# Rotating an 8192 x 8192 float32 matrix by 90 degrees: macro tiles of 3072 columns with three load and three store buffers, in place of tiles of 4096 columns with two and two

## The chip, the cores and the metric

The kernel runs on one core of one Trainium2 chip. The time is the device time of that core in microseconds (us), lower is better. "Packet" means one record of the DMA part of the trace: one contiguous piece that one of the core's 16 DMA engines reads and writes on, or the few bytes that report a completion.

## The reference

```python
def setup_inputs():
    return {"x": np.random.randn(8192, 8192).astype(np.float32), "k": 1}

def reference(x, k):
    return np.rot90(x, k)
```

There is nothing to compute: 268.44 MB are read and 268.44 MB are written. A rotation by 90 degrees is a transpose and a reversal of one axis.

## The kernel before

A macro tile is 1024 rows by C columns. It is loaded in blocks of 128 rows (RT = 8 blocks, q of them in one DMA). DVE (VectorE) copies each block into small chunks of 128 x 512 with the columns of each 128-block reversed; PE (TensorE) transposes 128 x 128 blocks into its output memory, PSUM; ACT (ScalarE) copies PSUM into a store buffer of four column blocks (G = 4), and a DMA writes that out. Loads are issued by SP (SyncE), stores by ACT: two queues over the same 16 engines.

```python
R = 1024; RT = R // P; W = 4096; CH = 512; G = 4; PW = 2
# whole_reads: a finalize hook that makes each store read its 16 KB per partition
# as one contiguous piece, though it writes four rows of 4 KB:
#     ap = [ap[0], [1, 1], [1, ap[1][1] * ap[2][1]]]
# macro_tiles: widths 4096, 4096; in the last strip 4096, 2048, 1024, 1024
a_pool = ctx.enter_context(tc.tile_pool(name="a_pool", bufs=2))   # loads
r_pool = ctx.enter_context(tc.tile_pool(name="r_pool", bufs=68))  # chunks
o_pool = ctx.enter_context(tc.tile_pool(name="o_pool", bufs=2))   # stores
...
for r0, c0, C in tiles:
    q = W // C
    for t0 in range(0, RT, q):
        a = o_pool.tile(...) if loads < 2 else a_pool.tile(...)
        loads += 1
        nc.sync.dma_start(out=a, in_=x[...])             # 2 MB
        ...                                              # DVE: chunks[t, j] <- a, reversed
    for g0 in range(0, C // P, G):
        ot = o_pool.tile([P, W], dt, tag="o")
        for h in range(0, G, PW):
            ...                                          # PE: needs chunks of ALL t (8 row blocks)
            nc.scalar.copy(o[...], ps[:])
            ...
            nc.scalar.dma_start(out=dst, in_=o[...])     # 2 MB
```

Of the kernel before, what the change touches and what calls it, by code (L numbers as in the profile page):

```python
# [2 lines left out]

# [5 lines left out]

P = 128  # L10




R = 1024
RT = R // P
W = 4096
CH = 512
G = 4
PW = 2  # L20


def whole_reads(nc):






    for fn in nc.m.functions:  # L30
        for block in fn.blocks:
            for n, ins in enumerate(block.instructions):
                if not isinstance(ins, mybir.InstDMACopy):
                    continue
                src = ins.ins[0]
                ap = [list(d) for d in src.ap]
                if len(ap) == 3 and ap[2][0] == 1 and ap[1][0] == ap[2][1]:
                    ap = [ap[0], [1, 1], [1, ap[1][1] * ap[2][1]]]
                    block.instructions[n] = copy.replace(
                        ins,  # L40
                        ins=[copy.replace(src, ap=ap)],
                        ant_dge_precooked=False,
                    )


def macro_tiles(N, M):

    for r0 in range(0, N, R):
        widths = [W] * (M // W)
        if r0 == 0:  # L50
            widths[:1] = [4096]
        if r0 + R == N:
            widths[-1:] = [2048, 1024, 1024]
        c0 = 0
        for C in widths:
            yield r0, c0, C
            c0 += C


@with_exitstack  # L60
def kernel(
    ctx: ExitStack,
    tc: tile.TileContext,
    x: bass.AP,
    k: bass.AP,
    out: bass.AP,
):
    nc = tc.nc
    assert k == 1, f"only k=1 supported, got {k}"
    nc.at_finalize(whole_reads)  # L70

    N, M = x.shape
    dt = x.dtype

    consts = ctx.enter_context(tc.tile_pool(name="consts", bufs=1))
    ident = consts.tile([P, P], dt)
    make_identity(nc, ident)

    a_pool = ctx.enter_context(tc.tile_pool(name="a_pool", bufs=2))
    r_pool = ctx.enter_context(tc.tile_pool(name="r_pool", bufs=68))  # L80
    o_pool = ctx.enter_context(tc.tile_pool(name="o_pool", bufs=2))
    psum_pool = ctx.enter_context(
        tc.tile_pool(name="psum", bufs=2, space=bass.MemoryType.PSUM)
    )

    tiles = list(macro_tiles(N, M))
    loads = 0
    for r0, c0, C in tiles:
        last = (r0, c0, C) == tiles[-1]
        q = W // C  # L90
        chunks = {}
        for t0 in range(0, RT, q):

            if loads < 2:
                a = o_pool.tile([P, W], dt, tag="o")
            else:
                a = a_pool.tile([P, W], dt, tag="a")
            loads += 1
            a = a.rearrange("r (q c) -> r q c", q=q)
            nc.sync.dma_start(  # L100
                out=a,
                in_=x[r0 + t0 * P : r0 + (t0 + q) * P, c0 : c0 + C].rearrange(
                    "(q r) c -> r q c", q=q
                ),
            )


            for u in range(q):
                for j in range(C // CH):
                    ar = r_pool.tile([P, CH // P, P], dt, tag="ar")  # L110
                    nc.vector.tensor_copy(  # L111
                        out=ar[:],
                        in_=a[:, u, j * CH : (j + 1) * CH].rearrange(
                            "r (b m) -> r b m", m=P
                        )[:, :, ::-1],
                    )
                    chunks[t0 + u, j] = ar

        for g0 in range(0, C // P, G):
            ot = o_pool.tile([P, W], dt, tag="o")  # L120
            o = ot.rearrange("m (g f) -> m g f", g=G)
            S = PW if last and g0 + G == C // P else G
            for h in range(0, G, PW):
                ps = psum_pool.tile([P, PW, R], mybir.dt.float32)
                for w in range(PW):
                    g = g0 + h + w
                    for t in range(RT):
                        nc.tensor.transpose(  # L128
                            ps[:, PW - 1 - w, t * P : (t + 1) * P],
                            chunks[t, g * P // CH][:, g % (CH // P), :],  # L130
                            ident,
                        )
                nc.scalar.copy(o[:, G - PW - h : G - h, :], ps[:])  # L133

                done = h + PW
                if done % S == 0:
                    top = M - c0 - (g0 + done) * P
                    dst = out[top : top + S * P, r0 : r0 + R].rearrange(
                        "(g m) f -> m g f", g=S
                    )  # L140
                    nc.scalar.dma_start(  # L141
                        out=dst, in_=o[:, G - done : G - done + S, :]
                    )


# [1 line left out]
_INS = ['x', 'k']  # L147
_OUTS = [((8192, 8192), 'float32')]

_NUMBERS = {'k': 1}  # L150


# [26 lines left out]
```

## Time and profile before

| | before |
|---|---|
| time, median | 1276.11 us |
| PE, ACT, DVE busy | 56, 37, 28% |
| DMA queues, share of 16 engines | 49.8% loads, 49.8% stores |
| rate from 100 to 1100 us | 428 GB/s |

Part of the profile page of the kernel before: busy time by engine, the rate in 40 equal slices of the span, and the DMA queues (q1 is the loads' queue, q10 the stores'; packets, MB, share of 16 engines' span).

```profile
PE 719.2 (56%) x4096; PEld 685.5 (54%) x4096; DVE 355.2 (28%) x1024; ACT 466.9 (37%) x257; POOL 0.7 (0%) x6
...
GB/s 375 366 427 427 427 428 431 429 428 428 430 428 430 428 427 429 429 429 429 427 427 427 429 427 428 427 427 429 428 427 426 424 423 429 427 425 422 420 408 338
...
q1 hardware_dynamic: 20480, 268.44, 49.8%
q10 hardware_dynamic: 18576, 268.44, 49.8%
```

The rate is flat at 427 to 431 in the first three quarters after the start and at 420 to 429 after that; it is low in the first two slices and in the last two. The two queues together cover 99.6% of the engines.

The longest waits of the kernel before (us in total, times, longest):

```profile
DVE ar L111 <- DMA a<-in_x_dram: 894.4, 128, 15.4
ACT ot L133 <- DMA out_dram<-ot: 733.5, 122, 11.4
```

The compute engines wait for DMA on both sides: DVE for each of the 128 loads, ACT for 122 stores to give a buffer back.

The DMA view of the kernel before between 300 and 360 us (same columns as above):

```profile
q10 hardware_dynamic: 878, 12.80, 50.2%
q1 hardware_dynamic: 880, 12.85, 50.0%
```

The busy table by stretches of the kernel before (last three columns: granted PE clock, DMA share, GB/s):

```profile
0.00:100.00 100.00, 34.94 (x192) 30.55 (x192) 36.07 (x104) 20.08 (x12) 0.70 (x6) 0.88 0.96 391
100.00:1100.00 1000.00, 583.64 (x3264) 559.44 (x3264) 283.05 (x816) 370.49 (x204) 0.00 (x0) 0.75 1.01 428
1180.00:1274.00 94.00, 51.52 (x360) 48.42 (x358) 16.65 (x48) 43.22 (x24) 0.00 (x0) 0.81 0.94 390
```

### The profile page before, as it was taken

The numbers are of one execution on the slowest core, as the hardware profiler recorded it, in microseconds if no ns is written. First come the engines' busy times: TensorE is split into PE (matmuls) and PEld (weight loads), VectorE is DVE, ScalarE is ACT, GpSimd is POOL, SyncE is SP. The second block draws the span as 40 slices with busy tenths as digits, with TensorE's granted clock in tenths as the row PEclk, the third lists the DMA queues.
The fourth block names the chain that finished last, engine by engine and source line by source line (L and its number), as shares of the span: only waits on it lengthen the run. The fifth ranks groups of instructions, "written<-read, shape, count | busy, mean of one in ns | idle before, by whom it ended". The sixth has DMA issues, their size and how long they took to land.

```text
span 1274.2 us, 10388 instructions
## 1 busy us (share of the span) xinstructions
PE 719.2 (56%) x4096; PEld 685.5 (54%) x4096; DVE 355.2 (28%) x1024; ACT 466.9 (37%) x257; POOL 0.7 (0%) x6
## 2 busy tenths in 40 slices
PE   1455556556655665556546565565565665665564
PEld 0355556555554655556546555565555554665564
DVE  4422232223222322232223222322232222321210
ACT  0233343334334333343334333433343333434444
POOL 0000000000000000000000000000000000000000
PEclk9968686877777677776886867768777778678878
DMA  9999999999999999999999999999999999999998
GB/s 375 366 427 427 427 428 431 429 428 428 430 428 430 428 427 429 429 429 429 427 427 427 429 427 428 427 427 429 428 427 426 424 423 429 427 425 422 420 408 338
DMA packets 39105, 537.55 MB, mean 422 GB/s; under 512 B 4112, under 2 KB 4112, under 8 KB 6160
## 3 DMA queue, kind: packets, MB, share of 16 engines
q1 hardware_dynamic: 20480, 268.44, 49.8%
q10 hardware_dynamic: 18576, 268.44, 49.8%
q8 instruction: 32, 0.52, 0.2%
q14 instruction: 17, 0.14, 0.0%
HBM read 268.44 MB, written 268.44 MB: 421 GB/s over the span
## 4 chain that ended last, share of the span: by engine, by line
DMA 84%; DVE 12%; issue 2%; ACT 1%; PE 0%; DVEq 0%; SPq 0%; ACTq 0%
DMA a<-in_x_dram 81%; DVE ar L111 12%; DMA out_dram<-ot 3%; ACT ot L133 1%; PE ps L128 0%; DVEq L111 0%; SPq L100 0%; ACTq L133 0%; ACTq L141 0%
## 5 line engine op out<-in xcount | busy, mean ns | idle before, releaser
L128 PE MATMUL ps<-ident,ar 128*128 128x128 f32 x4096 | 719.2, 358 | 543.8 <-ACT ot L133 500.2
L128 PEld LDWEIGHTS ps<-ident,ar 128*128 128x128 f32 x4096 | 685.5, 192 | 577.3 <-ACT ot L133 530.5
L133 ACT COPY ot<-ps 128x2048 f32<-128x2048 f32 x256 | 465.6, 1870 | 789.3 <-DMA out_dram<-ot 733.5
L111 DVE COPY ar<-a 128x512 f32<-128x512 f32 x1024 | 355.2, 421 | 894.4 <-DMA a<-in_x_dram 894.4
L133 ACT ACT_TABLE_LOAD x1 | 1.3, 1283 | 10.9 <-DVE ar L111 10.9
masks.py:199 POOL TENSOR_SCALAR_AFFINE_SELECT ident<-ident 128x128 f32<-128x128 f32 x1 | 0.3, 292 | 0.1
masks.py:197 POOL MEMSET ident<- 128x128 f32 x1 | 0.2, 204 | 0.3 <-POOLq L160 0.3
L160 POOL MEMSET const-bfloat16-1.0<- 128x1 bf16 x1 | 0.1, 102 | 0.0
L160 POOL MEMSET const-uint8-127<- 128x1 uint8 x1 | 0.1, 102 | 0.0
L160 POOL MEMSET const-float32-0.0<- 128x1 f32 x1 | 0.1, 99 | 0.2 <-issue 0.2
L160 POOL MEMSET const-float32-1.0<- 128x1 f32 x1 | 0.1, 99 | 0.0
## 6 DMA issues: line engine op xcount, KB each, us to landing
a<-in_x_dram SPq DMA_DIRECT2D x128, 2048.0 KB, 16.6
out_dram<-ot ACTq DMA_DIRECT2D x127, 2048.0 KB, 15.9
out_dram<-ot ACTq DMA_DIRECT2D x2, 1024.0 KB, 5.7
```

The costliest lines, as they stand in the source:

```text
L111: nc.vector.tensor_copy(out=ar[:], in_=a[:, u, j * CH : (j + 1) * CH].rearrange("r (b m) -> r b m", m=P)[:, :, ::-1],)
L128: nc.tensor.transpose(ps[:, PW - 1 - w, t * P : (t + 1) * P], chunks[t, g * P // CH][:, g % (CH // P), :], ident,)
L133: nc.scalar.copy(o[:, G - PW - h : G - h, :], ps[:])
L160: nc = _bacc.Bacc("TRN2", target_bir_lowering=False, num_devices=1)
```

## The change

The intent was more transfers in flight: smaller load buffers (12 KB per partition instead of 16) make room for three load and three store buffers. Core of the diff:

```diff
-W = 4096
+W = 3072
-        widths = [W] * (M // W)
+        widths = [3072, 3072, 2048]
         if r0 == 0:
-            widths[:1] = [4096]
+            widths = [2048, 3072, 3072]
         if r0 + R == N:
-            widths[-1:] = [2048, 1024, 1024]
+            widths = [3072, 3072, 1024, 1024]
...
-            yield r0, c0, C
+            yield r0, c0, C, max(1, 2048 // C)
...
-    a_pool = ctx.enter_context(tc.tile_pool(name="a_pool", bufs=2))
-    r_pool = ctx.enter_context(tc.tile_pool(name="r_pool", bufs=68))
-    o_pool = ctx.enter_context(tc.tile_pool(name="o_pool", bufs=2))
+    a_pool = ctx.enter_context(tc.tile_pool(name="a_pool", bufs=3))
+    r_pool = ctx.enter_context(tc.tile_pool(name="r_pool", bufs=60))
+    o_pool = ctx.enter_context(tc.tile_pool(name="o_pool", bufs=3))
...
-            if loads < 2:
+            if loads < 3:
```

So loads now come in packets of 12 KB (3072 columns) or 8 KB (2048 columns; 4 KB for the last two tiles), while a store is still 2 MB in packets of 16 KB.

More of the change, by code (lines that the diff above doesn't have):

```diff
@@ L48, in macro_tiles @@
     for r0 in range(0, N, R):
-        widths = [W] * (M // W)
+        widths = [3072, 3072, 2048]
         if r0 == 0:
-            widths[:1] = [4096]
+            widths = [2048, 3072, 3072]
         if r0 + R == N:
-            widths[-1:] = [2048, 1024, 1024]
+            widths = [3072, 3072, 1024, 1024]
+        assert sum(widths) == M
         c0 = 0
         for C in widths:
-            yield r0, c0, C
+            yield r0, c0, C, max(1, 2048 // C)
             c0 += C
@@ L87 @@
     loads = 0
-    for r0, c0, C in tiles:
-        last = (r0, c0, C) == tiles[-1]
-        q = W // C
+    for r0, c0, C, q in tiles:
+        last = (r0, c0, C, q) == tiles[-1]
         chunks = {}
         for t0 in range(0, RT, q):
-            if loads < 2:
-                a = o_pool.tile([P, W], dt, tag="o")
+            if loads < 3:
+                a = o_pool.tile([P, G * R], dt, tag="o")
             else:
@@ L98 @@
             loads += 1
-            a = a.rearrange("r (q c) -> r q c", q=q)
+            a = a[:, : q * C].rearrange("r (q c) -> r q c", q=q)
             nc.sync.dma_start(
@@ L119 @@
         for g0 in range(0, C // P, G):
-            ot = o_pool.tile([P, W], dt, tag="o")
+            ot = o_pool.tile([P, G * R], dt, tag="o")
             o = ot.rearrange("m (g f) -> m g f", g=G)
```

## The prediction

> **What bounds the kernel now.** It only moves data: the DMA packets of the loads and of the stores each cover 49.8% of 16 engines' span (page, queues). In the middle (windows, 100 to 1000 us) the rate is flat at 427 to 429 GB/s with DMA share 1.01. A 16 KB packet takes 611 ns (median of the trace's packet records), and 16 x 16,384 B / 611 ns = 429 GB/s: the engines have no gap to fill. The Trainium skill, "DMA: Bandwidth & Descriptors", section "Where 436 GB/s comes from", gives a ceiling of 435.2 GB/s; the trace agrees, its packets paying a few ns each on top. PE, ACT and DVE are at 56, 37 and 28%. DVE waits 894 us for loads, ACT 733 us for stores to free a buffer (waits). Two loads and two stores in flight cycle in 19.5 us (16.6 us load + 2.8 us DVE), so in steady state another transfer always stands behind the one that lands. A third buffer there buys nothing.
>
> Time is lost only at the ends:
> - Head: from 16 to 60 us the DMA moved 16.2 MB where 429 GB/s would move 18.9: 6.2 us lost. Loads run alone with two buffers, and one in flight during the 2.8 us copy is too little (landings 5.4 to 7.1 us apart instead of 4.9, timeline). 60 to 80 us: another 0.7 us.
> - Tail: from 1200 us on, about 3 MB short, 7 us; ACT waits there for store buffers (34.7 us).
>
> **What the change does.**
> - Removes most of the head's loss. The first tile is 2048 columns, eight 1 MB loads, three in flight; three loads of 2.4 us outlast the 1.4 us copy plus about 2 us of start latency. 28 spare chunks let the next tile's loads run on. Gain 5 to 6 us.
> - Removes part of the tail's loss: three stores queued cover the last tile's DVE, PE and ACT work. Gain 2 to 5 us.
> - Adds packets. Medians are 611, 309 and 159 ns for 16, 8 and 4 KB: about 7.5 ns per packet beside the bytes. Seven strips cut rows in three, not two: 448 more packets per engine, 3.4 us; 64 more loads add a 9 ns semaphore packet each, 0.6 us. Cost 4 us, all on the critical path. Stores are unchanged.
> - Moves: smaller load packets take turns with 16 KB store packets, so stores get the larger share while both are queued. Nothing is lost as long as a load is always queued; three buffers and 12 spare chunks ensure that. No change in time.
> - Copies, transposes and evictions keep their counts.
>
> **Sum.** 1276 - 5.5 - 4 + 4 = about 1270.5 us. Range 1262 to 1280. Chance of faster by over 2%: 0.01 (under 1250.4 us, while 537 MB at 429 GB/s take 1253). Within 2%: 0.96. Slower by over 2%: 0.03.
>
> **What would show it.** Steady windows at 425 to 428 GB/s, a little under before; 12 KB packets of about 460 ns. The page's first slices rising from 375 and 366 to 400 or more and about 425; the last above 338. ACT still waiting on stores and DVE on loads, by hundreds of us. Longer landing times of loads (near 22 us for 1.5 MB) without a higher rate.
>
> **What would make it wrong.** 12 KB rows might be split into smaller packets, or meet the memory less evenly, and the steady rate drop by over 1%. Loads starved by the stores' larger share could leave the last tile waiting. Or tile changes could starve the loads for want of chunks, seen as dips in the middle slices.

## More of the kernel before

The three rounds of experiments ran on three chips, and the kernel before ran again in each round; the ratios are against that.

One thing to keep: a store needs columns from all eight row blocks, so the first store of a tile cannot be made before the last load of that tile has landed.

After the start, the stores are never short of data, and the loads never of room, for long.

## The result

The changed kernel took 1286.16 us (median of 4 runs, 1285.05 to 1287.2) beside 1276.11 us of the kernel before: slower by 0.8%. The ratio is 1.008, 95% interval 1.0063 to 1.0098. (Ratios here are the mean time of one kernel's runs over that of the other's in the same rounds, so not quite the ratio of the medians.)

The lines of the page of the changed kernel that answer to those above:

```profile
PE 629.0 (49%) x4096; PEld 585.8 (46%) x4096; DVE 360.9 (28%) x1024; ACT 469.6 (37%) x257; POOL 0.7 (0%) x6
...
GB/s 391 419 428 430 427 428 427 426 411 407 428 429 425 400 420 427 426 418 403 419 427 426 419 410 420 427 426 416 416 421 425 424 407 408 425 429 427 402 416 368
...
q1 hardware_dynamic: 28672, 268.45, 50.2%
q10 hardware_dynamic: 18576, 268.44, 49.4%
```

The first two slices rose, nearly as far as forecast. But the middle is no longer flat: every five slices or so, that is once per strip of 1024 rows, the rate dips to between 400 and 416.

The table by stretches of the changed kernel:

```profile
0.00:100.00 100.00, 42.57 (x269) 35.85 (x270) 36.68 (x104) 30.59 (x17) 0.70 (x6) 0.81 0.99 414
100.00:1100.00 1000.00, 488.60 (x3189) 458.22 (x3187) 281.18 (x798) 362.10 (x198) 0.00 (x0) 0.74 1.00 420
1180.00:1285.00 105.00, 56.78 (x384) 52.99 (x384) 19.87 (x56) 47.67 (x26) 0.00 (x0) 0.74 0.96 400
```

In the head, 23 GB/s more over 100 us are 2.3 MB, or 5.4 us gained at 429 GB/s. In the middle, 8 GB/s less over 1000 us are 8 MB, or 19 us lost. At the end, 94 us at 390 GB/s fall short of 429 by 8.5 us, and 105 us at 400 GB/s by 7.1 us: 1.4 us gained. The sum is +12 us; the two spans differ by 11.2.

The longest waits of the changed kernel on the same two engines:

```profile
DVE ar L111 <- DMA a<-in_x_dram: 819.4, 176, 10.3
...
ACT ot L133 <- DMA a<-in_x_dram: 429.8, 38, 17.6
ACT ot L133 <- PE ps L128: 222.0, 74, 28.2
...
ACT ot L133 <- DMA out_dram<-ot: 116.4, 36, 6.2
...
DVE ar L111 <- PE ps L128: 85.5, 16, 6.5
```

ACT hardly waits for store buffers any more (116 us instead of 734). It waits for *loads*, and for PE, which in turn waits for loads. The stores run short of data. There are two candidates in these lines: ACT, which does nothing with a load, is held by one 38 times; and the stores may simply be too far ahead.

The timeline of the changed kernel at one dip (start, duration, engine, instruction; in brackets the idle time before and what ended it) shows the first:

```profile
407.77 1.87 ACT L133 COPY ot<-ps 128x2048 f32<-128x2048 f32 x1 [0.92 <-PE ps L128]
409.64 1.43 DVE L111 COPY ar<-a 128x512 f32<-128x512 f32 x4 [5.26 <-DMA a<-in_x_dram]
...
416.98 1.43 DVE L111 COPY ar<-a 128x512 f32<-128x512 f32 x4 [5.91 <-DMA a<-in_x_dram]
419.43 0.55 ACTq L141 DMA_DIRECT2D out_dram<-ot  x1
419.45 1.43 DVE L111 COPY ar<-a 128x512 f32<-128x512 f32 x4 [1.03 <-DMA a<-in_x_dram]
```

ACT finished the copy for a store at 409.64 us, but the store was issued at 419.43, together with the landing of a load. The list of the compiled instructions says why: the scheduler deals eight completion semaphores (counters that a DMA raises when it has landed) to all DMAs in the order of its own schedule, and a DMA waits until the one that had the semaphore before it has landed. In the kernel before, loads and stores alternate one to one, so loads nearly always get the same four semaphores and stores the other four, and only 9 of 129 stores come after a load on their semaphore. With 8 loads to 6 stores (or to 4) they mix, and 97 of 129 stores carry a wait for a load.

### The profile page after: what moved, and what is told of

Same layout as the page of the kernel before. It is cut to its first block, busy times and chain, and to the rows that moved or that the text cites. A ratio compares the mean times of both kernels' runs of the same rounds, so it can differ in the third digit from the quotient of the medians.

```text
span 1285.4 us, 10702 instructions
## 1 busy us (share of the span) xinstructions
PE 629.0 (49%) x4096; PEld 585.8 (46%) x4096; DVE 360.9 (28%) x1024; ACT 469.6 (37%) x257; POOL 0.7 (0%) x6
## 4 chain that ended last, share of the span: by engine, by line
DMA 85%; DVE 8%; PE 4%; ACT 2%; issue 1%; ACTq 0%; DVEq 0%; SPq 0%
DMA a<-in_x_dram 84%; DVE ar L111 8%; PE ps L128 4%; ACT ot L133 2%; DMA out_dram<-ot 1%; ACTq L141 0%; DVEq L111 0%; SPq L100 0%; DVEq L174 0%; ACTq L133 0%
## 5 line engine op out<-in xcount | busy, mean ns | idle before, releaser
L128 PE MATMUL ps<-ident,ar 128*128 128x128 f32 x4096 | 629.0, 325 | 645.8 <-ACT ot L133 512.1
L128 PEld LDWEIGHTS ps<-ident,ar 128*128 128x128 f32 x4096 | 585.8, 171 | 688.8 <-ACT ot L133 544.0
L111 DVE COPY ar<-a 128x512 f32<-128x512 f32 x1024 | 360.9, 420 | 904.9 <-DMA a<-in_x_dram 819.4
```

The source lines that it names most:

```text
L111: nc.vector.tensor_copy(out=ar[:], in_=a[:, u, j * CH : (j + 1) * CH].rearrange("r (b m) -> r b m", m=P)[:, :, ::-1],)
L128: nc.tensor.transpose(ps[:, PW - 1 - w, t * P : (t + 1) * P], chunks[t, g * P // CH][:, g % (CH // P), :], ident,)
```

## The experiments

### First round: the shared semaphores

First theory: these false waits are the loss. Rivals: 60 chunks are too few where tiles change (DVE waits 85.5 us for PE), or the 12 and 8 KB packets of the loads get too small a share of the engines beside 16 KB packets of the stores.

**after_own.** The changed kernel with a finalize hook (a function that edits the finished instruction list) that gives the loads four of the eight semaphores and the stores the other four. Waits are rewritten so that each engine still waits for the transfers that it needs.

```diff
+    nc.at_finalize(own_semaphores)
...
+ load = i.engine == mybir.EngineType.SP
+ new = half[load][count[load] % 4]      # half: four ids for loads, four for stores
... # each old wait is rewritten to the new semaphore and count of the same DMA;
... # a wait that only served the turn on a shared semaphore is dropped
```

> The changed kernel, instruction for instruction, but loads count on four completion semaphores of their own and stores on the four others. Theory (a store that is ready must wait for an unrelated load that had its turn on the same semaphore): ACT's 430 us of waits on loads vanish, the dips to 400 GB/s between 200 and 1100 us vanish, the time falls from 1286 to 1268-1274 us. Rival 1 (60 chunks are too few at the tile changes: DVE waits 85 us for PE) and rival 2 (12 and 8 KB load packets get too small a share beside 16 KB store packets): dips stay, 1283-1288 us.

Measured: 1294.67 us, ratio 1.0145 (1.012 to 1.0171). The false waits were gone and the kernel was *slower* than the changed kernel (1286.16 us). The rate and waits of after_own:

```profile
GB/s 391 419 425 428 426 424 411 426 428 408 427 403 424 411 426 424 414 429 425 427 429 427 423 427 425 420 414 426 429 425 407 413 422 425 424 427 427 423 425 258
```

```profile
ACT ot L196 <- PE ps L191: 547.8, 77, 33.6
...
ACT ot L196 <- DMA out_dram<-ot: 241.0, 51, 7.7
...
ACT ot L196 <- DMA a<-in_x_dram: 0.8, 1, 0.8
```

The waits on loads at ACT fell from 430 to 0.8 us, yet the dips stayed. ACT now waits for PE, and the timeline shows for what (after_own, one dip):

```profile
354.59 6.21 PE L191 MATMUL ps<-ident,ar 128*128 128x128 f32 x41 [3.19 <-DVE ar L174]
...
356.81 1.87 ACT L196 COPY ot<-ps 128x2048 f32<-128x2048 f32 x1 [28.50 <-PE ps L191]
...
361.00 0.55 ACTq L204 DMA_DIRECT2D out_dram<-ot  x1
```

ACT stood idle for 28.5 us until the last load of the next tile had landed, been copied and been transposed. All stores of the tile before had long been issued. The DMA view of after_own for 350 to 365 us holds loads alone:

```profile
q1 hardware_dynamic: 520, 5.63, 98.8%
```

That is 375 GB/s (5.63 MB in 15 us), not 429. The table by stretches has for the middle of after_own:

```profile
100.00:1100.00 1000.00, 469.66 (x3210) 426.69 (x3209) 279.31 (x792) 366.48 (x201) 0.00 (x0) 0.73 1.01 422
```

So my first theory fell: the false waits are real, but without them the middle rose only from 420 to 422 GB/s, some 4 or 5 of the 19 us. That the whole time grew is another matter: the last slice of the page fell from 368 to 258 GB/s, about 8 us of work, and the control shows a like fall.

**before_own**, the control: the same hook in the kernel before.

> Control: the same regrouping of the semaphores in the kernel before, where loads and stores alternate and hardly ever share one. All theories: 1275-1277 us, no change. A clear gain would say that the regrouping does something else.

Measured: 1279.48 us, ratio 1.0028 (1.0013 to 1.0043), a little slower than expected. Its rate:

```profile
GB/s 371 359 427 430 428 431 428 428 430 428 430 428 428 430 429 429 427 429 427 429 429 425 430 427 430 427 426 424 431 427 429 424 426 424 425 430 419 428 421 269
```

The middle is unchanged (428 GB/s from 100 to 1100 us); the last slice fell from 338 to 269. In the last strip the loads of the kernel before come in 8 and 4 KB, and with the hook the last of them is copied later (at 1255.9 instead of 1246.8 us). So the hook itself costs time at the end. I did not follow this further; below, kernels with the hook are compared with this one.

**eq.** As many stores as loads in each tile, with the same packet sizes on both sides (but for the last two tiles, 4 KB loads against 8 KB stores). The cut leaves out that PSUM buffers went from 2 to 4, as PW went from 2 to 1:

```diff
-G = 4
-PW = 2
+GM = 3
+PW = 1
...
+        G = C // P * q // RT      # 3 column blocks per store for 3072, 2 for 2048 and 1024
```

> The changed kernel with as many stores as loads in each tile (3 or 2 column blocks per store instead of 4), semaphores as the scheduler deals them. Only 22 of the stores then carry a wait on a load's semaphore instead of 97. Theory: most of the dips vanish, but smaller store packets cost 3-5 us: 1270-1280 us. Rival 1 (chunks): dips at the tile changes stay, 1286-1292 us. Rival 2 (shares): also predicts a gain, since load and store packets are equal now; so this run alone doesn't tell it from the theory.

Measured: 1280.29 us, ratio 1.0037 (1.0022 to 1.0052): better than the change, but dips remain, of another kind (DVE waits 289 us for PE). The premise was wrong: by the semaphores in the trace of this run, 95 of its 193 stores come after a load on their semaphore, not 22. Its rate:

```profile
GB/s 383 428 429 429 428 429 429 426 423 429 427 427 427 426 429 428 417 417 427 428 427 406 415 427 429 428 403 415 429 428 429 417 409 428 429 428 402 406 394 364
```

**before_wait.** The kernel before with its own semaphores, every third store waiting on purpose for the load before last:

```diff
+ if stores % 3 == 0 and len(loads) > 8:
+     _, new, value = loads[-2]
+     need[new] = max(need.get(new, 0), value)
```

> The kernel before (own semaphores), and every third store is made to wait for the load before last in the program, as stores of the changed kernel do by chance. Theory: each of about 40 stores is held about 8 us, the store queue runs dry, and the time grows from 1276 to 1285-1320 us, with ACT waiting on loads for hundreds of us. Rivals 1 and 2: such a wait is not what costs; 1274-1280 us.

Measured: 1283.11 us, ratio 1.0051 (1.0034 to 1.0068). A miss of the expectation, and no good test: ACT waited for a load only 3 times (28.8 us), because the load waited for had usually landed already. It adds 3.6 us to before_own and settles nothing.

### Second round: the share of the queues

New theory. The 16 engines serve the load queue and the store queue in turn, one packet each. Then the *bytes* are shared as the packet sizes are. The DMA view of the changed kernel, first from 305 to 320 us (12 KB loads), then from 402 to 414 us (8 KB loads):

```profile
q10 hardware_dynamic: 250, 3.83, 59.7%
q1 hardware_dynamic: 245, 2.64, 41.4%
```

```profile
q10 hardware_dynamic: 227, 3.44, 67.6%
q1 hardware_dynamic: 227, 1.63, 32.2%
```

The packet counts are equal (227 and 227, of which 45 only report completions) and the bytes are not (3.44 and 1.63 MB). The Trainium skill, "DMA: Bandwidth & Descriptors", section "Queues, rings and completion order", says that each engine round-robins between its queues at packet granularity; these counts agree, with one contiguous read per turn. While both queues hold work, the stores of the changed kernel get 60 to 68% of the engines. But over a tile, loads and stores need the same bytes. So the stores finish early, no new store can be made before the last of the eight loads of the next tile lands, and the loads are left alone. Right after, from 414 to 420 us:

```profile
q1 hardware_dynamic: 241, 1.72, 73.1%
q10 hardware_dynamic: 33, 0.29, 11.7%
```

The engines were busy for 85% of this stretch, at 336 GB/s.

How often this happens can be counted in the packet records of the traces: stretches of over 3 us in which no packet of a store starts. The kernel before has 1 (4.8 us); the changed kernel has 31, 187 us in all, in which the DMA moved 396 GB/s. Against 428 that is a shortfall of about 14 us (an estimate from these figures), beside the 10 us by which the kernel is slower.

The test is to change packet sizes and nothing else, in both directions.

**before_8_16.** In before_own, each load of 16 KB per partition is read in two pieces of 8 KB. Buffers, tiles, transfers and stores are as before.

```diff
+ elif len(ap) == 2 and ap[1] == [1, 4096]:       # loads in pieces of 8 KB, both sides
+     two = lambda t: copy.replace(t, ap=[list(t.ap[0]), [2048, 2], [1, 2048]])
```

> Kernel before with own semaphores (1279.5 us), but each load is read in pieces of 8 KB, stores stay at 16 KB. New theory (the queues take turns packet by packet, so smaller load packets give the stores the larger share; stores then finish a tile's work early, the store queue runs dry, and the loads alone cannot fill the engines): beyond the packets' own cost (960 more per engine, 7.2 us, so 1287) phases of loads alone and dips of the rate appear, 1291-1315 us. If only packets cost: 1285-1289 us, flat.

Measured: 1326.85 us, ratio 1.039 (1.0365 to 1.0416), more than expected, and 47 us over before_own. Its rate and waits:

```profile
GB/s 370 350 428 378 415 424 385 421 402 414 427 383 420 396 414 424 384 428 394 411 423 390 423 390 416 422 373 423 400 417 426 384 426 391 415 426 398 420 426 352
```

```profile
ACT ot L206 <- DMA out_dram<-ot: 416.2, 79, 9.3
...
ACT ot L206 <- PE ps L201: 414.1, 49, 38.7
```

The dips of the change, deeper, in the kernel before: ACT waits 414 us for PE, where before_own waited 75. The DMA view for 374 to 382 us of this run has loads alone:

```profile
q1 hardware_dynamic: 281, 2.17, 71.6%
```

Stretches of over 3 us without a store packet: 14, 231 us in all, at 356 GB/s, an estimated shortfall of 39 of the 47 us.

**before_8_8.** The same with stores read in 8 KB pieces too.

```diff
- ap = [ap[0], [1, 1], [1, ap[1][1] * ap[2][1]]]
+ ap = [ap[0], [2048, 2], [1, 2048]] if ap[1][1] == 4 else ...
```

> The same with stores cut to 8 KB reads too, so that packets are equal again. Share theory: no phases of loads alone, a flat rate, 1279.5 + 15 us of packet cost = 1290-1297 us, so hardly more, or less, than the kernel with unequal packets although it has more packets. If small packets themselves do the harm: clearly slower than the unequal one, by 7 us or more.

Measured: 1283.5 us, ratio 1.0047 (1.0019 to 1.0075). It has more packets than before_8_16 and is 43 us faster. Its rate is flat again:

```profile
GB/s 373 356 428 427 427 426 427 422 426 427 427 426 428 427 427 427 424 427 428 426 426 424 426 426 425 424 425 424 424 426 422 417 425 426 424 424 426 412 371 369
```

It has no stretch of over 3 us without a store packet. It is the unequal sizes that cost, not small packets. Packets themselves are cheap: 960 more for loads and 1016 for stores on each engine cost 4.0 us over before_own, 2 ns each, not the 7.5 ns by which their durations differ. I had expected 15 us. The 4.0 us are loose, though: the two kernels ran in different rounds, and by their ratios they differ by 2.4 us, within the intervals. In the middle alone the rate fell from 428 to 425 GB/s, 7 us for some 1,600 packets per engine, and the end was better than the control's (last slice 369 against 269). So a fair estimate is 1 to 4 ns per packet.

**after_own_s8.** The change with own semaphores and one edit: stores read in 8 KB pieces (the line above). Now no load packet is smaller than a store packet, but for the last strip.

> The changed kernel with own semaphores (1291-1295 us), stores read in pieces of 8 KB, loads at 12 and 8 KB. Share theory: stores no longer get more than loads, the dips of 18 us vanish, packets cost 7.7 us more: 1276-1285 us. If the share is not the cause: 1298-1303 us.

Measured: 1273.99 us, ratio 0.9977 (0.9955 to 0.9999), 20.7 us less than after_own, and below the range I gave. No stretch of over 3 us without a store packet is left, where after_own had 17 (207 us).

**eq_own.** Equal counts, equal packet sizes and own semaphores.

> As many stores as loads of the same packet size in each tile, and own semaphores for both. If share and shared semaphores together are what cost: the dips of the version with scheduler's semaphores (14 us) vanish, 1267-1275 us. If the 60 chunks are what costs at the tile changes (there DVE waited 289 us for PE): dips stay, 1278-1286 us.

Measured: 1280.07 us, ratio 1.0025 (1.0003 to 1.0047). The dips of the middle are gone, but I had expected 1267 to 1275 us: the end is worse, as in the control.

```profile
GB/s 386 427 429 430 427 428 429 426 426 428 428 429 427 426 428 429 429 424 425 427 427 424 422 421 429 428 422 421 425 426 427 423 421 422 426 423 423 408 422 283
```

So here, with equal packets, the shared semaphores did make dips (eq against eq_own: 424 and 426 GB/s from 100 to 1100 us), though the total came out the same.

### Third round: what is left of the semaphores and of the third buffer, and a better kernel

**after_s8.** The changed kernel with its semaphores as dealt and the one edit of the stores.

> The changed kernel as it stands, semaphores as the scheduler deals them (97 stores carry a wait on a load's semaphore), and one edit: stores are read in pieces of 8 KB. If the share of the queues is the whole cause of the loss: as with own semaphores, 1272-1277 us. If shared semaphores cost something of their own once the share is right: 1278-1285 us, with ACT waiting on loads.

Measured: 1274.08 us, ratio 0.9984 (0.9972 to 0.9997). As with own semaphores, although 97 stores still carry the wait. Rate, middle and waits:

```profile
GB/s 392 421 427 429 428 429 428 426 429 427 429 427 427 428 428 428 428 425 428 428 429 421 424 429 427 426 423 423 429 427 425 418 427 430 421 419 422 424 404 335
```

```profile
100.00:1100.00 1000.00, 538.07 (x3189) 513.77 (x3188) 287.12 (x817) 359.92 (x198) 0.00 (x0) 0.76 1.01 427
```

```profile
ACT ot L133 <- DMA out_dram<-ot: 722.3, 115, 9.5
...
DVE ar L111 <- PE ps L128: 571.6, 95, 10.1
...
DVE ar L111 <- DMA a<-in_x_dram: 307.6, 91, 6.1
ACT ot L133 <- PE ps L128: 64.8, 14, 18.0
```

The picture is turned round: the middle is back at 427 GB/s, no stretch of over 3 us lacks store packets, ACT waits for store buffers as in the kernel before and never for a load, and the loads run ahead until DVE waits for a free chunk. DVE waits 572 us for PE here, against 85.5 in the change, and the kernel is 12 us faster: so the rival that blamed the lack of chunks falls too. Here the loads have the larger packets (12 against 8 KB), so the two sides are not equal, but the side that runs ahead is now the harmless one: loads that run ahead stop by themselves and leave a full store queue; stores that run ahead leave an empty one.

**after_s8_b2.** after_s8 with two load and two store buffers (`bufs=2` twice, `loads < 2`).

> The same with two buffers for loads and two for stores instead of three and three. The prediction held that a third buffer buys nothing in steady state and only helps at the ends: then the windows from 100 to 1100 us stay within 1% of the version with three, and the time grows by 3-8 us (head and tail), 1276-1284 us. If depth matters in the middle: dips, over 1285 us.

Measured: 1284.67 us, ratio 1.007 (1.0057 to 1.0084). The third buffers are worth 10.6 us here. By stretches, 0 to 100 us fell from 414 to 387 GB/s (6 us), and 100 to 1100 us from 427 to 424 (7 us, within the 1% I gave, but not nothing); some came back at the end.

**before_head.** The kernel before with one edit, the useful part of the change by itself: four loads in flight while the store buffers have nothing else to do.

```diff
-            if loads < 2:
+            if loads < RT and loads % 4 < 2:
```

> The kernel before with one edit: the first tile's eight loads use the two store buffers and the two load buffers in turn, so four are in flight while there is nothing to store. Packets stay 16 KB on both sides. The head's loss of 6 us should vanish: the second slice of the page rises from 366 to over 415 GB/s, 1269-1273 us.

Measured: 1272.08 us, ratio 0.9969 (0.9956 to 0.9981). The fastest of the kernels with before_head_tail, though by 0.3% only. Its second slice is 395, not over 415 as I had written.

```profile
GB/s 399 395 429 430 428 428 429 430 427 430 428 429 428 429 428 428 428 429 428 425 424 428 429 429 429 425 425 428 427 427 427 426 420 423 427 424 423 424 409 342
```

**before_head_tail.** That, and in the last strip stores in 8 KB and then 4 KB pieces, as the loads there.

```diff
+ if stores > 120: continue                         # leave 4 KB
+ elif stores > 112: ap = [ap[0], [2048, 2], [1, 2048]]
```

> That, and in the last strip stores are read in pieces as small as the loads beside them (8 KB, then 4 KB). The share theory also explains the tail of the kernel before, whose last loads come in 8 and 4 KB packets against 16 KB stores: 2-5 us less than the version with the head alone, 1265-1271 us. If the tail is bound by something else, the extra packets cost 1-3 us: 1271-1275 us.

Measured: 1271.8 us, ratio 0.997 (0.9957 to 0.9982): the same as before_head. Balancing the tail bought nothing; what bounds the last 40 us stays open.

## Why the prediction was right or wrong

- *What bounds the kernel*: right. The kernels here that keep both queues filled run at 424 to 428 GB/s from 100 to 1100 us, and none passes that.
- *Head, 5 to 6 us gained*: right, 5.4 us, and for the reason given: with two buffers the gain was gone (387 against 414 GB/s in after_s8_b2). before_head gets most of it alone, 3.8 us.
- *Tail, 2 to 5 us gained*: about 1.4 us, so too much.
- *Packets, 4 us lost on the critical path*: too much. I took differences of packet durations as time. Where two queues overlap on an engine, 1976 more packets per engine cost 4.0 us (before_8_8 against before_own), an estimated 1 to 4 ns each; the change's 448 are then an estimated 0.5 to 2 us.
- *"Moves: smaller load packets take turns with 16 KB store packets, so stores get the larger share while both are queued. Nothing is lost as long as a load is always queued ... No change in time"*: this is the step that failed. The fact was seen and its consequence waved away. That a load is always queued was nearly true, and not enough: the stores ran out, the next tile's first store needs the tile's last load, and loads alone with three buffers moved 336 to 375 GB/s in the stretches shown. It cost most of the 19 us lost between 100 and 1100 us: cutting the stores alone (after_s8) brought the middle from 420 to 427 GB/s, 16 us. ACT's waits for store buffers, forecast to stay at hundreds of us, fell to 116. Three pairs show the cause: 16 KB loads cut to 8 KB cost the kernel before 47 us; cutting the stores too gave 43 of them back; cutting the stores of the change gave it 12 us.
- *"A third buffer there buys nothing"*: not tested in the kernel before. In the changed shape with stores cut to 8 KB, third buffers on both sides bought about 0.7% in the middle.
- *What would make it wrong*: "loads starved by the stores' larger share" was named, but for the last tile only; the dips in the middle were named for want of chunks, which was not the cause.

After the result I also first blamed the shared semaphores, because the trace named them in the longest new wait. Taking them away gave the middle some 4 or 5 us and lost more at the end. With the share put right, they cost nothing measurable (1274.08 against 1273.99 us). Why the loads alone move less in those stretches was not tested. The traces show two things there. Packets take longer: from 350 to 365 us in after_own they cover 98.8% of the engines, but a 12 KB packet took 516 ns in the mean, where it took 461 beside stores (after, 305 to 320 us). And engines stand empty: from 374 to 382 us in before_8_16 only 71.6% is covered. At one landing in after_own the completion counts of the 16 engines came between 362.0 and 366.6 us, so a load is as late as its slowest engine. These are observations and not experiments.

## What to carry to other kernels

When a load queue and a store queue both keep the DMA engines busy, compare their packet sizes: engines alternate packet by packet, so the side with larger contiguous reads gets more bytes, and if a barrier (here: all loads of a tile before its first store) ties the two, the smaller side stalls both. Keep the packets equal, or let the side that must come first have the larger ones, even by cutting the other side's. Both held here, in one kernel and with pieces of 8 to 16 KB. And when a new wait tops the list, take it away before believing it, and read the stage that you meant to mend, not only the total: here ACT's wait for loads fell from 430 to 0.8 us and the middle gained 2 of the 8 GB/s that it had lost.

## What the Trainium skill lacked or had wrong

- "DMA: Bandwidth & Descriptors", "Queues, rings and completion order": it has the round-robin by packet, but not that the bytes are then shared by packet size. The runs show 227 packets each and 3.44 against 1.63 MB in 12 us, and a cost of 3.9% in total time over the kernel before (before_8_16). Its packet holds some 9 to 17 descriptors; here the turn changed with every contiguous read of 8 to 16 KB.
- The same page, "Rules for kernel authors", advises coalescing many small transfers into one large one. It has no rule for the contiguous pieces inside a large transfer beside another busy queue: with the stores' transfers left at 2 MB, reading the stores in 8 instead of 16 KB pieces took the changed kernel from 1286.2 to 1274.1 us.
- The same page, "Why small descriptors are slow (HBM only)", gives a fixed overhead per packet. The durations show one too (611 ns for 16 KB, 309 for 8 KB, so 7 ns). What the page does not say is how much of it is left when two queues keep the engines busy: there the time grew by an estimated 1 to 4 ns per packet (before_8_8).
- No page says that a wait dealt with a shared completion semaphore can name a transfer that has nothing to do with the waiting one: 97 of 129 stores carried one, 38 times ACT's idle time ended on a load, up to 17.6 us.
